# Five feed-forward stages by Strassen's seven products in a two-block transformer kernel

## Chip, cores and metric

One Trainium2 chip, one core. The metric is device microseconds of the whole program, median over runs.

## The reference, cut to what matters

Two transformer blocks follow one another on x of 512 tokens and 1024 features in fp32: a first block (sparse attention, a linear recurrence, a gated merge) with one feed-forward, then two layers of four-way mixed attention ("mix"), each between two feed-forwards. Five feed-forwards in all, each of the form

```
h = rms_norm(x, g)
x = x + half * (silu(h @ w_gate) * (h @ w_up)) @ w_down
```

with 1024 features and 2816 hidden ones; half is 1 in the first block and 0.5 later. After the feed-forward that ends a layer, x itself is normalized once more (`final_norm`).

## The kernel before, in words

Activations stand with features on the 128 partitions: xT is [128, 8, 512], eight feature tiles of 512 tokens. To keep fp32 accuracy, each operand of a matmul is split into a high part (rounded by a ScalarE copy to fp32r) and a low part (VectorE: the value less its high part), and a product is three matmuls: high by high, high by low, low by high (`feat`, L144 to 152).

`stream` (L116) loads weights in pieces of [128, 1024], 512 KB (L126, on SyncE's queue), casts 512 columns at a time to `hi` (L133, ScalarE) and subtracts to `lo` (L135, VectorE; GpSimd while a mix runs). Its tiles raw (2 buffers), hi and lo (4 each) are of the pool `wp`, opened once for the whole kernel, so the weights of a stage can be loaded and split while the stage before still computes.

`ffn` (L515) opens a pool `ph_f`. For each of 11 units of 256 hidden features it streams the gate's and the up's block and makes for each 2 x 8 x 3 = 48 matmuls of 512 columns; from PSUM, VectorE multiplies by the norm's factor rB (L531, L537), ScalarE takes Silu (L532), VectorE multiplies both (L538) and the result is split into fh and fl (L219, L220), 22 tiles each of ph_f. Then down: for each of four pairs of output tiles 22 x 2 x 3 = 132 matmuls in two PSUM banks, added to xT (L547 or L549). Behind each xT tile, the next stage's norm squares it, adds the square to acc on GpSimd (L233) and splits the scaled tile to xh and xl (L237, L238); at the end `norm_r` or, behind the second feed-forward of a layer, `final_norm` makes the row factors: a sum over partitions on TensorE (L203), a power on GpSimd (L196), a broadcast on TensorE (L212) and a copy (L215). `final_norm` then multiplies all eight xT tiles by rF, a tile of ph_f (L620).

The order on each engine is written down ahead of the run by a planner that follows program order, priorities (`high_priority`) and its own estimate of durations; on the chip each engine keeps to that order. Pools are placed as on a stack: `mix` opens ph_x, `ffn` opens ph_f, one after the other at the same depth. PSUM has eight banks; tags mm, s and t have two each.

Of the kernel before, what the change touches and what calls it, by code (L numbers as in the profile page):

```python
# [8 lines left out]
FT = mybir.dt.float32  # L9
# [9 lines left out]
T = 512  # L19
# [73 lines left out]
class Kern:  # L93
# [212 lines left out]
    def block1(self):  # L306
# [35 lines left out]
        with tc.tile_pool(name="ph_m", bufs=1, side="right") as pm:  # L342
            mh, ml = pm.tile([128, 8, T], FR, name="mh"), pm.tile([128, 8, T], FR, name="ml")
            skews = self.skews(pm)
            next(skews)
            with left_, tc.tile_pool(name="ph_t", bufs=1) as pt:
                self.merge(pt, got, ah, al, lh, ll, mh, ml)
            px = self.st.enter_context(tc.tile_pool(name="xT", bufs=1))
            self.xT = xT = px.tile([128, 8, T], FT, name="xT")
            nc.sync.dma_start(xT, I["xT"])  # L350
            whole(skews)
            self.outproj(I["w_o"], mh, ml, self.norm("norm2", 0))
        self.dump("x1", xT)
        self.ffn(0, None, self.norm("ffn1", 0))
        self.dump("x2", xT)
# [5 lines left out]
    def norm(self, gname, g0):  # L361

        xh, xl = self.new_x()
        acc = self.new_acc()
        xT = self.xT

        def tile_done(k):
            self.norm_k(xT[:, k], k, self.col(gname, g0 + k), xh, xl, acc)

        def finish():  # L370
            self.xh, self.xl = xh, xl
            self.r, self.rB = self.norm_r(acc)
        return tile_done, finish
# [141 lines left out]
    def ffn(self, f, half, norm):  # L515

        tc, nc, I = self.tc, self.nc, self.I
        V, S, G = nc.vector, nc.scalar, nc.gpsimd
        xh, xl, rB, xT = self.xh, self.xl, self.rB, self.xT
        ks = [(k, k) for k in range(8)]  # L520
        with tc.tile_pool(name="ph_f", bufs=1) as pf:
            self.pf = pf
            fh = [pf.tile([128, n, T], FR, name=f"fh{i}") for i, n in enumerate((8, 8, 6))]
            fl = [pf.tile([128, n, T], FR, name=f"fl{i}") for i, n in enumerate((8, 8, 6))]
            for j in range(11):
                wg = self.stream(I["w_g"][f, j], 8, 256)
                wu = self.stream(I["w_u"][f, j], 8, 256)
                z = [pf.tile([128, T], FT, tag="z", name="z", bufs=3) for m in range(2)]
                ps = self.feat2(wg, ks, lambda k: xh[:, k], lambda k: xl[:, k])
                for m in range(2):  # L530
                    V.tensor_mul(z[m], ps[m], rB)  # L531
                    S.activation(z[m], z[m], AF.Silu)  # L532
                ps = self.feat2(wu, ks, lambda k: xh[:, k], lambda k: xl[:, k])
                for m in range(2):
                    k = 2 * j + m
                    u = pf.tile([128, T], FT, tag="u", name="u", bufs=2)
                    V.tensor_mul(u, ps[m], rB)  # L537
                    V.tensor_mul(u, u, z[m])  # L538
                    self.split(fh[k // 8][:, k % 8], fl[k // 8][:, k % 8], u)
            for j in range(4):  # L540
                w = self.stream(I["w_d"][f, j], 22, 256)
                ps = self.feat2(w, [(k, k) for k in range(22)], lambda k: fh[k // 8][:, k % 8],
                                lambda k: fl[k // 8][:, k % 8])
                for m in range(2):
                    k = 2 * j + m
                    if half is None:
                        V.tensor_add(xT[:, k], ps[m], xT[:, k])  # L547
                    else:
                        V.scalar_tensor_tensor(xT[:, k], ps[m], half, xT[:, k], op0=OP.mult, op1=OP.add)  # L549
                    norm[0](k)  # L550
            norm[1]()


    def block2(self):
# [3 lines left out]
        for l in range(2):  # L558
            self.dump(f"xf1_{l}", xT)
            norm = self.norm("ffn2", 8 * l)  # L560
            self.wide = False
# [10 lines left out]
    def final_norm(self, l):  # L572
# [6 lines left out]
        if not last:  # L579
            xh, xl = self.new_x()  # L580
            acc2 = []
            gg = self.sm.tile([128, 8], FT, tag="gg", name="gg")
            V.tensor_mul(gg, self.col("final", 8 * l, 8), self.col("ffn1", 8 * l + 8, 8))

        def tile_done(k):
# [10 lines left out]
            if k == 0:  # L596
                acc2.append(self.pf.tile([128, T], FT, name="acc2"))
# [3 lines left out]
            g = gg[:, k:k + 1]  # L601
            S.activation(xh[:, k, :], xk, AF.Copy, scale=g)
            V.scalar_tensor_tensor(xl[:, k, :], xk, g, xh[:, k, :].bitcast(FT), op0=OP.mult, op1=OP.subtract)

        def finish():
            rf = self.rstd(self.tokred(acc, self.ones, 1), 1024, 4, "rt")
            if not last:
# [5 lines left out]
                self.r, self.rB = r, self.bcast(r)  # L613
                self.xh, self.xl = xh, xl
            rB = self.bcast(rf, self.pf, "rF")
            for k in range(8):
# [9 lines left out]
    def mix(self, px, l, norm):  # L626
# [12 lines left out]
        def hot():  # L639
            return tc.high_priority(offset=1000)  # L640

        rows = tl("rows2", [128, ROWS["_2"]])
        nc.sync.dma_start(rows, I["rows2"][l].partition_broadcast(128))
# [27 lines left out]
        def sqp():  # L671
            return tl("sqp", [128, T], FT, 2)

# [94 lines left out]
        def ptile():  # L768
            return tl("P", [128, T], FT, 8)

# [81 lines left out]
        def wout_b(Y, sum_b):  # L852
# [14 lines left out]
            for j in range(4):  # L867
# [3 lines left out]
                for m in range(2):  # L871
                    k = 2 * j + m
                    with hot():
                        t = sqp()
                        V.tensor_mul(t, banks[j][m], rb)
                        V.tensor_add(xT[:, k], t, xT[:, k])
                        norm[0](k)


        def diff():  # L880
# [29 lines left out]
            def head(h):  # L910
# [31 lines left out]
                def soft(qb):  # L942
# [4 lines left out]
                    for m in range(2):  # L947
# [3 lines left out]
                        PE.matmul(ps, qT[:96, qb * 128:qb * 128 + 128], kT[:96], start=True, stop=True)  # L951
                        p = tl("P1", [128, T], FT, 2) if m else ptile()
                        V.tensor_tensor_reduce(p, ps, t["toep"][:, 384 - qb * 128:896 - qb * 128], 1.0, 3e38,
# [82 lines left out]
        def na():  # L1036
# [6 lines left out]
            def evac(tb, ps, rt):  # L1043
                v = tl("sqp", [128, 4, 128], FR, 2, name="vst")
                vevac(v, v4(ps), rt)
# [17 lines left out]
            def head(h):  # L1063
# [21 lines left out]
                def soft(cb):  # L1085
# [4 lines left out]
                    mn, sm, rc = (t["st"][:, i, cb:cb + 1] for i in range(3))  # L1090
                    B = tl("P1", [128, 8, 32], FT, 2, name="nab")
                    G.tensor_tensor(B, namask[:, cb, None, :].to_broadcast([128, 8, 32]), t["E"][:, :, o:o + 32],
# [588 lines left out]
def host(inputs):  # L1681
# [94 lines left out]
    for i, n in enumerate(("w_g", "w_u", "w_d")):  # L1776
        A[n] = np.stack([blocks(f[i], 256) for f in ff])
    A["rows2"] = np.stack([np.concatenate([x["mla_q_norm_2"][l][64:], x["mla_k_norm_2"][l][64:], x["gqa_q_norm_2"][l],
# [54 lines left out]
```

## Time and profile before

| | |
|---|---|
| median of 3 runs | 3131.63 us (3128.5 to 3133.9) |
| the profiled execution | 3132.92 us |
| its span, first to last instruction | 3131.1 us |
| mean granted TensorE clock | 0.983 |
| share of the span busy: PE, DVE, ACT, POOL | 97%, 55%, 44%, 24% |

Matmuls are pipelined, so the records of one engine overlap; the pace of matmuls is the distance of their starts. Idle time of an engine is noted with what ended it.

### The profile page before, as it was taken

How to read it: one execution, taken by the hardware profiler on the slowest of the kernel's cores; microseconds unless marked ns; L12 is line 12 of the kernel's file. 1: busy time of each engine (PE TensorE's matmuls, PEld its weight loads, DVE VectorE, ACT ScalarE, POOL GpSimd, SP SyncE). 2: the span in 40 equal slices, each digit the busy share in tenths (PEclk: the TensorE clock that was granted, in tenths of full speed). 3: DMA queues.
4: the chain of work that ended last, by engine and by line, in shares of the span. 5: the costliest groups of instructions: out<-in, count | busy, mean ns of one | idle time of the engine just before them, and what ended most of it. 6: DMA issues, size and time to landing. Idle time of an engine off the chain costs nothing.

```text
span 3131.1 us, 41177 instructions
## 1 busy us (share of the span) xinstructions
PE 3030.5 (97%) x15289; PEld 2549.3 (81%) x15289; DVE 1721.3 (55%) x3167; ACT 1389.4 (44%) x2707; POOL 736.7 (24%) x699
## 2 busy tenths in 40 slices
PE   7999999999999999999888999999999998999998
PEld 6888877888888888889877888888888987778886
DVE  7576785454444454337786554355443488665433
ACT  4577774343333333236765333333332577543322
POOL 0466650010000000028853000010000877210000
PEclk9999999999999999999989999999999998999999
DMA  4311112342333323333211323323233321122232
GB/s 135 105 60 58 48 41 76 100 143 95 100 98 91 101 95 95 101 112 100 79 32 41 101 95 98 99 89 99 97 96 97 111 90 47 41 88 94 95 101 81
DMA packets 105265, 275.81 MB, mean 88 GB/s; under 512 B 27172, under 2 KB 36900, under 8 KB 104904
## 3 DMA queue, kind: packets, MB, share of 16 engines
q1 hardware_dynamic: 105064, 273.18, 28.1%
q8 instruction: 120, 1.97, 0.3%
q14 instruction: 81, 0.66, 0.1%
HBM read 268.93 MB, written 6.80 MB: 88 GB/s over the span
## 4 chain that ended last, share of the span: by engine, by line
PE 73%; issue 13%; DVE 7%; ACT 3%; POOL 3%; DMA 1%; SPq 0%; DVEq 0%; POOLq 0%; ACTq 0%
PE ps_mm L150 7%; PE ps_mm L152 7%; PE ps_mm L151 7%; PE ps_s L151 6%; PE ps_s L150 6%; PE ps_s L152 6%; PE ps_t L152 6%; PE ps_t L150 6%; PE ps_t L151 6%; PE ps_mm L180 2%; PE ps_mm L181 2%; PE ps_mm L182 2%; DVE PTl L220 1%; PE ps_t L792 1%; POOL lo L135 1%
## 5 line engine op out<-in xcount | busy, mean ns | idle before, releaser
L133 ACT ACTIVATE hi<-raw 128x512 fp32r<-128x512 f32 (+4 forms) x952 | 594.5, 627 | 1362.0 <-PE ps_mm L151 410.5
L135 DVE TENSOR_TENSOR lo<-raw,hi 128x512 fp32r<-128x512 f32 (+1 forms) x782 | 547.0, 701 | 934.1 <-ACT hi L133 925.5
L150 PE MATMUL ps_mm<-xh,hi 128*128 128x512 f32 x784 | 309.8, 395 | 1.4 <-ACT hi L133 1.2
L152 PE MATMUL ps_mm<-xh,lo 128*128 128x512 f32 x784 | 307.0, 394 | 3.1 <-POOL lo L135 3.1
L151 PE MATMUL ps_mm<-xl,hi 128*128 128x512 f32 x784 | 307.7, 392 | 0.0
L233 POOL TENSOR_TENSOR acc<-acc,sq 128x512 f32<-128x512 f32 x42 | 62.5, 1488 | 1037.8 <-issue 525.7
L152 PE MATMUL ps_s<-xh,lo 128*128 128x512 f32 (+1 forms) x664 | 259.7, 392 | 6.3 <-DVE lo L135 6.3
L150 PE MATMUL ps_s<-xh,hi 128*128 128x512 f32 (+1 forms) x664 | 256.9, 392 | 7.4 <-ACT hi L133 7.4
L151 PE MATMUL ps_s<-xl,hi 128*128 128x512 f32 (+1 forms) x664 | 260.6, 392 | 3.0 <-DVE xl L238 2.9
L181 PE MATMUL ps_mm<-lo,xh 128*128 128x256 f32 (+1 forms) x896 | 255.9, 288 | 2.0 <-DVE lo L135 2.0
L180 PE MATMUL ps_mm<-hi,xh 128*128 128x256 f32 (+1 forms) x896 | 255.4, 289 | 1.3 <-ACT tk L661 1.0
L182 PE MATMUL ps_mm<-hi,xl 128*128 128x256 f32 (+1 forms) x896 | 253.7, 286 | 0.1
L135 POOL TENSOR_TENSOR lo<-raw,hi 128x512 fp32r<-128x512 f32 (+2 forms) x170 | 225.5, 1334 | 114.6 <-ACT hi L133 107.9
L150 PE MATMUL ps_t<-xh,hi 128*128 128x512 f32 x608 | 236.9, 390 | 0.0
L151 PE MATMUL ps_t<-xl,hi 128*128 128x512 f32 x608 | 236.7, 389 | 0.0
L152 PE MATMUL ps_t<-xh,lo 128*128 128x512 f32 x608 | 235.9, 390 | 0.3 <-DVE lo L135 0.3
L152 PEld LDWEIGHTS ps_mm<-xh,lo 128*128 128x128 f32 x784 | 148.2, 189 | 35.1 <-POOL lo L135 4.1
L180 PEld LDWEIGHTS ps_mm<-hi,xh 128*128 128x128 f32 x896 | 171.9, 193 | 5.0 <-issue 1.7
L181 PEld LDWEIGHTS ps_mm<-lo,xh 128*128 128x128 f32 x896 | 172.5, 193 | 4.0 <-DVE lo L135 2.5
L150 PEld LDWEIGHTS ps_mm<-xh,hi 128*128 128x128 f32 x784 | 148.6, 190 | 32.9 <-ACT hi L133 1.9
L182 PEld LDWEIGHTS ps_mm<-hi,xl 128*128 128x128 f32 x896 | 171.9, 193 | 1.7 <-DVE xl L238 0.5
L151 PEld LDWEIGHTS ps_mm<-xl,hi 128*128 128x128 f32 x784 | 148.7, 190 | 30.1
(526 smaller groups left out, 6646.7 us busy)
## 6 DMA issues: line engine op xcount, KB each, us to landing
raw<-in_w_g SPq DMA_DIRECT2D x110, 512.0 KB
raw<-in_w_u SPq DMA_DIRECT2D x110, 512.0 KB
raw<-in_w_d SPq DMA_DIRECT2D x108, 512.0 KB
raw<-in_w_o SPq DMA_DIRECT2D x24, 512.0 KB
raw<-in_w_c SPq DMA_DIRECT2D x16, 512.0 KB
raw<-in_w_m SPq DMA_DIRECT2D x16, 512.0 KB
raw<-in_w_a SPq DMA_DIRECT2D x12, 512.0 KB
raw<-in_w_d SPq DMA_DIRECT2D x20, 256.0 KB
```

The lines of the kernel that those rows point to most:

```text
L133: nc.scalar.activation(hi[:, :c], x, AF.Copy)
L135: eng.tensor_tensor(lo[:, :c], x, hi[:, :c].bitcast(FT), op=OP.subtract)
L150: mm(ps, wh, mh(km), start=s, stop=False)
L151: mm(ps, wh, ml(km), start=False, stop=False)
L152: mm(ps, wl, mh(km), start=False, stop=e)
L180: mm(out[tb], h, wh, start=k == 0 and tb % 2 == 0, stop=False)
L181: mm(out[tb], h, wl, start=False, stop=False)
L182: mm(out[tb], o, wh, start=False, stop=k == K - 1 and tb % 2 == 1)
L220: self.nc.vector.tensor_sub(lo, src, hi.bitcast(FT))
L233: (eng or nc.gpsimd).tensor_tensor(acc, acc, sq, op=OP.add)
L792: PE.transpose(ps[:, qb * 128:qb * 128 + 128], P[qb][:, kb * 128:kb * 128 + 128], ident)
```

## The change

All five feed-forwards compute gate and up in Winograd's form of Strassen's scheme. Per unit, the weights are four blocks a11, a12, a21, a22 (row: which of the unit's two hidden tiles, gate beside up; column: even or odd feature tiles), each [128, 1024], 512 KB. The activations are four blocks too (even or odd feature tile, first or second half of the tokens), and of them seven combinations are made once per stage by `combine`, which takes the place of `norm_split` ahead of every feed-forward: per pair of feature tiles two scaled copies, four subtractions of 256 columns, and the splits. Seven products of 24 matmuls with 256 columns each take the place of 96 matmuls with 512 columns.

- Weight sums: s1 = a21 + a22 and s3 = a21 - a11 by accumulating DMAs issued by GpSimd, s2 = s1 - a11 and s4 = a12 - s2 on VectorE.
- Low parts: of products 3 (a12) and 6 (a22) by a ScalarE copy of the negated high part and an accumulating DMA; of the other five by VectorE.
- The products lie in banks mm and s; VectorE, ScalarE and GpSimd combine them to the tiles c, and `act` does the multiplication by rB, Silu, the product (GpSimd) and the split.
- The tiles raw2 (a11, a22), S (the sums), wh and wl (high and low parts, 3 buffers each), c and fh, fl (8 each instead of 22) are of ph_f. a12 and the down weights go through `wp`.
- Down runs in five passes over 4, 4, 4, 4 and 6 hidden tiles, put between the products of the units after, each adding to xT.
- In the first unit the first three products issue the first three quarters of the features ahead of the last quarter.
- `combine` has its tiles x and t in the pool of the stage before: ph_o, ph_x (tq, tk) or ph_f (c). `final_norm` has acc2 and rF in buffers of S and raw2.
- A pool x3, open from the first feed-forward on, holds the three additional blocks; in `mix` the buffers P, P1 and sqp move into it, with the same counts.

```diff
+    def combine(self, k, xk, g, xc):
+        V, S = self.nc.vector, self.nc.scalar
+        p = k // 2
...
+        S.activation(x[:, 2 * (k % 2):2 * (k % 2) + 2], xk.rearrange("p (a b) -> p a b", a=2), AF.Copy, scale=g)
+        if k % 2 == 0:
+            self.split(hi[0][:, p, 0], lo[0][:, p, 0], x[:, 0])
+            return
+        self.split(hi[0][:, p, 1:3], lo[0][:, p, 1:3], x[:, 2:4])
+        t = self.t4("t")
+        V.tensor_sub(t[:, 0], x[:, 1], x[:, 0])
+        V.tensor_sub(t[:, 1], x[:, 3], t[:, 0])
+        V.tensor_sub(t[:, 2], x[:, 3], x[:, 1])
+        V.tensor_sub(t[:, 3], x[:, 2], t[:, 1])
+        self.split(hi[0][:, p, 3], lo[0][:, p, 3], t[:, 0])
+        self.split(hi[1][:, p], lo[1][:, p], t[:, 1:4])
...
     def ffn(self, f, half, norm):
...
+            def load(u, i):
+                pool, tag, n = (pf, "raw2", 3) if i % 3 == 0 else (pf, "S", 4) if i == 2 else (self.wp, "raw", 2)
+                t = pool.tile([128, 2 * T], FT, tag=tag, name=f"A{i}", bufs=n)
+                with tc.high_priority(offset=6000):
+                    nc.sync.dma_start(t, I["w_gu"][f, u, i])
+                return t
+            def prod(x, c, ranges=((0, 4),), dma=False):
+                h, o = (pf.tile([128, 2 * T], FR, tag=n, name=n, bufs=3) for n in ("wh", "wl"))
+                with tc.high_priority(offset=3000):
+                    S.activation(h, x, AF.Copy)
+                    if dma:
+                        S.activation(o, x, AF.Copy, scale=-1.0)
+                        G.dma_start(o, x, accum_op=OP.add)
+                    else:
+                        V.tensor_sub(o, x, h.bitcast(FT))
+                nbank[0] += 1
+                ps = self.bank(("mm", "s")[nbank[0] % 2])
+                for a, b in ranges:
+                    for i in range(2):
+                        out = ps[:, i * 256:i * 256 + 256]
+                        for p in range(a, b):
+                            sl = slice((4 * i + p) * 128, (4 * i + p) * 128 + 128)
+                            mm(out, h[:, sl], xh[c](p), start=i == 0 and p == 0, stop=False)
+                            mm(out, h[:, sl], xl[c](p), start=False, stop=False)
+                            mm(out, o[:, sl], xh[c](p), start=False, stop=i == 1 and p == 3)
+                    yield
...
+            def unit(u):
+                a11, s1, a22 = load(u, 0), load(u, 2), load(u, 3)
+                s2, s3 = stile(), stile()
+                with early():
+                    G.dma_start(s1, a22, accum_op=OP.add)
+                    S.activation(s3, a11, AF.Copy, scale=-1.0)
+                    G.dma_start(s3, I["w_gu"][f, u, 2], accum_op=OP.add)
+                    V.tensor_sub(s2, s1, a11)
+                r = ((0, 3), (3, 4)) if u == 0 else ((0, 4),)
+                heads = [prod(x, c, r) for x, c in ((a11, 0), (s1, 3), (s2, 4))]
...
+            d = iter(())
+            for u in range(11):
+                if u % 2 == 0 and u:
+                    d = down(list(range(2 * u - 4, 2 * u + (0 if u < 10 else 2))), u == 10)
+                for i, _ in enumerate(unit(u)):
+                    if i in ((2, 6) if u < 10 else (2,)):
+                        next(d, None)
+            whole(d)
             norm[1]()
```

## Rows read from the trace of the kernel before

**Rows 1.** The page, part 1: busy time, share and instructions of each engine.

```profile
PE 3030.5 (97%) x15289; PEld 2549.3 (81%) x15289; DVE 1721.3 (55%) x3167; ACT 1389.4 (44%) x2707; POOL 736.7 (24%) x699
```

**Rows 2.** Windows: stretch, its length, busy time of each engine, granted clock, DMA share, GB/s.

```profile
800.00:1000.00 200.00, 200.00 (x884) 165.63 (x883) 87.31 (x128) 62.86 (x104) 4.28 (x3) 1.00 0.32 97
...
1020.00:1050.00 30.00, 30.00 (x142) 25.09 (x141) 12.77 (x18) 10.22 (x17) 4.02 (x3) 1.00 0.27 92
```

**Rows 3.** Timeline of PE, first feed-forward: start us, us, what; ten consecutive matmuls.

```profile
899.84 0.39 PE L150 MATMUL ps_mm<-xh,hi 128*128 128x512 f32 x1
...
901.88 0.39 PE L150 MATMUL ps_mm<-xh,hi 128*128 128x512 f32 x1
```

**Rows 4.** Timeline of PE, projections of the first mix: 27 consecutive matmuls.

```profile
1429.77 0.28 PE L180 MATMUL ps_mm<-hi,xh 128*128 128x256 f32 x1
...
1432.88 0.28 PE L182 MATMUL ps_mm<-hi,xl 128*128 128x256 f32 x1
```

**Rows 5.** Groups by line and form: xcount, busy us, mean ns of one, idle before.

```profile
L133 ACT ACTIVATE hi<-raw 128x512 fp32r<-128x512 f32 x934 | 586.9, 631 | 1350.4 <-PE ps_mm L151 410.5 <-PE ps_s L151 403.6 <-PE ps_t L151 401.5
L135 DVE TENSOR_TENSOR lo<-raw,hi 128x512 fp32r<-128x512 f32 x776 | 545.4, 705 | 932.8 <-ACT hi L133 924.3 <-PE ps_t L152 2.2
...
L220 DVE TENSOR_TENSOR PTl<-ps_t,PTh 128x256 fp32r<-128x256 f32 x32 | 13.4, 418 | 13.2 <-ACT PTh L219 12.7
```

**Rows 6.** Instructions of a line, 1024 columns: ns min/median/max, first and last start us.

```profile
L502 ACT ACTIVATE yT<-yT x4: 1059/1060/1061, 166.7 to 413.4; 128x1024 f32<-128x1024 f32 x4
...
L704 DVE TENSOR_TENSOR tk<-tk,rk x2: 1226/1226/1227, 1426.0 to 2470.3; 128x1024 f32<-128x1024 f32 x2
```

**Rows 7.** The same view of lines 238 and 233.

```profile
L238 DVE SCALAR_TENSOR_TENSOR xl<-xT,cols,xh x48: 734/1324/1780, 638.0 to 2765.3; 128x512 fp32r<-128x512 f32 x48
...
L233 POOL TENSOR_TENSOR acc<-acc,sq x42: 1284/1542/1673, 638.5 to 2764.8; 128x512 f32<-128x512 f32 x42
```

**Rows 8.** The page, part 3: DMA queue, packets, MB, share of 16 engines' span.

```profile
q1 hardware_dynamic: 105064, 273.18, 28.1%
```

**Rows 9.** The chain that ended last, 70 to 110 us: start us, us, transfer.

```profile
74.65 4.06 DMA raw<-in_w
...
81.23 3.94 DMA raw<-in_w_lx
```

**Rows 10.** Timelines of ACT and DVE, entry of the fourth feed-forward.

```profile
2094.68 0.59 ACT L215 COPY rB<-ps_n 128x512 f32<-128x512 f32 x1 [0.94 <-PE ps_n L212]
...
2097.42 0.69 DVE L135 TENSOR_TENSOR lo<-raw,hi 128x512 fp32r<-128x512 f32 x1 [2.96 <-ACT hi L133]
...
2101.21 5.39 DVE L620 SCALAR_TENSOR_TENSOR xT<-xT,cols,rF 128x512 f32<-128x512 f32 x8 [0.38 <-ACT rF L215]
...
2107.72 1.28 DVE L531 TENSOR_TENSOR z<-ps_mm,rB 128x512 f32<-128x512 f32 x2
```

**Rows 11.** Timelines of PE and SP, entry of the second mix.

```profile
2434.83 0.39 PE L152 MATMUL ps_s<-fh,lo 128*128 128x512 f32 x1
...
2435.25 0.33 SPq L643 DMA_DIRECT2D rows<-in_rows  x1
```

**Rows 12.** Timeline of PE, end of the second mix: the last output matmul.

```profile
2748.20 0.63 PE L152 MATMUL ps_mm<-yhl,lo 128*128 128x512 f32 x1
```

**Rows 13.** Windows of 5 us, entry of the fifth feed-forward; columns as in rows 2.

```profile
2745.00:2750.00 5.00, 5.00 (x14) 3.87 (x14) 5.00 (x6) 3.13 (x6) 3.28 (x2) 0.59 0.00 0
2750.00:2755.00 5.00, 4.25 (x17) 2.85 (x16) 5.00 (x8) 2.85 (x5) 1.85 (x2) 1.00 0.00 0
2755.00:2760.00 5.00, 4.11 (x17) 2.75 (x16) 5.00 (x6) 2.45 (x5) 2.78 (x2) 1.00 0.39 108
```

**Rows 14.** Timelines of PE, POOL and ACT, end of the third feed-forward.

```profile
2086.52 0.94 PE L203 MATMUL ps_n<-ones,acc 128*128 128x1 f32 x8
...
2088.01 1.46 POOL L196 TENSOR_TENSOR rt<-nm,mhalf 128x4 f32<-128x4 f32 x1 [4.72 <-DVE nm L194]
...
2099.50 1.05 PE L212 MATMUL ps_n<-ident,rt 128*128 128x128 f32 x8
2100.59 0.59 ACT L215 COPY rF<-ps_n 128x512 f32<-128x512 f32 x1 [0.49 <-PE ps_n L212]
```

More of the change, by code (lines that the diff above doesn't have):

```diff
@@ L517, in ffn @@
         tc, nc, I = self.tc, self.nc, self.I
[L518 to L520 removed]
+        V, S, G, mm = nc.vector, nc.scalar, nc.gpsimd, nc.tensor.matmul
+        rB, xT = self.rB, self.xT
         with tc.tile_pool(name="ph_f", bufs=1) as pf:
             self.pf = pf
[L523 to L547, printed above, removed]
[L548 to L550 removed]
@@ new lines, in unit @@
+            def unit(u):
[8 more added lines that the diff above has]
+                heads = [prod(x, c, r) for x, c in ((a11, 0), (s1, 3), (s2, 4))]
+                c1, c2 = (pf.tile([128, 2, 2, 256], FT, tag="c", name="c", bufs=3) for _ in range(2))
+                if u == 0:
+                    for g in heads:
+                        next(g)
+                ps = whole(heads[0])
+                with soon():
+                    S.copy(c1[:, 0], ps)
+                yield
+                ps = whole(heads[1])
+                with soon():
+                    S.copy(c2[:, 1], ps)
+                yield
+                ps = whole(heads[2])
+                with soon():
+                    V.tensor_add(c1[:, 1], ps, c1[:, 0])
+                yield
+                a12 = load(u, 1)
+                ps = whole(prod(a12, 1, dma=True))
+                with soon():
+                    V.tensor_add(c1[:, 0], ps, c1[:, 0])
+                yield
+                ps = whole(prod(s3, 5))
+                with soon():
+                    V.tensor_sub(c2[:, 0], c1[:, 1], ps)
+                    G.tensor_tensor(c1[:, 1], c1[:, 1], c2[:, 1], op=OP.add)
+                    G.tensor_tensor(c2[:, 1], c2[:, 1], c2[:, 0], op=OP.add)
+                yield
+                s4 = stile()
+                with early():
+                    V.tensor_sub(s4, a12, s2)
+                ps = whole(prod(s4, 2))
+                with soon():
+                    V.tensor_add(c1[:, 1], ps, c1[:, 1])
+                    act(u, 0, c1)
+                yield
+                ps = whole(prod(a22, 6, dma=True))
+                with soon():
+                    V.tensor_add(c2[:, 0], ps, c2[:, 0])
+                    act(u, 1, c2)
+                yield
@@ new lines, in down, with run @@
+            def down(part, last):
+                n = len(part)
+                w, banks = {}, {}
+                def run(j, a, b, tag="t"):
+                    if j not in w:
+                        w[j] = self.stream(I["w_d"][f, j][:, part[0] * 256:(part[-1] + 1) * 256], n, 256)
+                        banks[j] = [self.bank(tag) for _ in range(2)]
+                    for i in range(a, b):
+                        for m in range(2):
+                            self.feat(banks[j][m], lambda k: pick(w[j](k), m), [(i, part[i])], lambda k: fh[k],
+                                      lambda k: fl[k], start=i == 0, stop=i == n - 1)
+                    if b < n:
+                        return
+                    for m in range(2):
+                        k = 2 * j + m
+                        V.scalar_tensor_tensor(xT[:, k], banks[j][m], 1.0 if half is None else half, xT[:, k],
+                                               op0=OP.mult, op1=OP.add)
+                        if last:
+                            norm[0](k)
+                if not last:
+                    for j in range(4):
+                        run(j, 0, n)
+                        yield
+                    return
+                run(0, 0, 4)
+                yield
+                run(1, 0, 4, "mm")
+                run(2, 0, 4, "s")
+                for j in range(3):
+                    run(j, 4, n)
+                run(3, 0, n)
```

82 lines of the change are left out of this document (63 added, 19 removed).

## Prediction

> **What bounds the kernel now.** I read the page's busy line first. TensorE (PE) is busy 97% of the span, VectorE (DVE) 55%, ScalarE (ACT) 44%, GpSimd (POOL) 24% [rows 1]. Then a window inside the first feed-forward (FFN): PE has no gap in 200 us at a granted clock of 1.00, DVE is busy 44% and ACT 31% of it; the window over the step from the first FFN to the second has no gap either [rows 2]. So in the five FFNs only the number and the pace of the matmuls count, and a weight transfer or a cast costs nothing while it stays ahead. The pace is read from start to start in the PE timeline, not from the 0.39 or 0.28 us of a record, which overlap. With 512 columns it is (901.88 - 899.84) / 9 = 226.7 ns [rows 3]; with 256 columns, in the projections of a mix stage, (1432.88 - 1429.77) / 26 = 119.6 ns [rows 4]. Two halves cost 239.2 ns, 5.5% more than a whole one.
>
> **What is removed.** Gate and up are 11 units of 96 matmuls of 512 columns, 1056 x 226.7 = 239.4 us of an FFN. They become 11 units of seven products of 24 matmuls with 256 columns, 1848 x 119.6 = 221.0 us. Seven eighths of the columns would be 12.5% less, the shorter matmuls leave 7.7%: 18.4 us of an FFN, **92 us of five**. Down keeps its 528 matmuls; in five passes instead of one they take as long. The Trainium skill, TensorE: Matmul & The Clock Gate, Back-to-back issue gap, has columns / 2.4 GHz plus 2.5 ns for a matmul: 215.8 and 109.2 ns. By that rule the gain would be 26 us of an FFN, 130 of five, and the sum below 38 us lower; the two rows are some 11 ns above it at both sizes, and I go by the rows.
>
> **What a unit adds on the other engines.** A unit with its share of down is 168 x 119.6 + 48 x 226.7 ns = 31.0 us of PE. A 1024-wide cast is 1.06 us on ACT, a 1024-wide subtraction 1.23 us on DVE [rows 6]; 512-wide ones 0.63 and 0.70 [rows 5].
> - ACT: 7 high parts, 2 negated copies, 1 negated block, at 1.06; 2 copies from PSUM, 2 Silu, 2 casts of the result and 4 of down at 0.63: 16.9 us, 55%.
> - DVE: 5 low parts, 2 weight sums and 2 scalings at 1.23; 5 combinations, 2 low parts, 4 of down, 3.6 additions to xT at 0.70: 21.3 us, 69%. Additions to xT are 40 instead of 8 an FFN.
> - POOL: 4 operations of 512 columns at 1.54 [rows 7] and 4 DMA issues. While POOL works on two tensors, DVE instructions on two tensors stretch: 0.73 us alone, median 1.32, 1.78 at worst [rows 7]. With 6.2 us of that, DVE comes to some 25 us, 82%.
> - DMA: 3.0 MB loaded and 2.0 MB accumulated. The queue moved 273 MB in 28.1% of the span, 310 GB/s while at work [rows 8]; 31 us hold 9.6 MB, enough even if an accumulated byte counts double.
>
> On average all stay under PE, so the steady state is hidden but for one wait. The low parts of products 3 (a12) and 6 (a22) come by accumulating DMA: two ACT copies, 2.1 us, then the transfer, and PE needs it at its third matmul. There are three buffers of high and low parts. Ahead of product 6 stand two products, 48 x 119.6 ns = 5.7 us, from the time its buffer is free; ahead of product 3 also a down pass of 5.4 us, from the third unit on. No DMA of POOL is in the trace. The nearest row is a 512 KB load on SP, 3.94 to 4.06 us from release to landing [rows 9]; as the accumulation reads two streams I bound it by that and by twice that. The stall of a unit then lies between 2.1 + 4.0 - 5.7 = 0.4 us and 4.4 us, or nothing where the down pass is put ahead. I take the row it is nearest to, 0.4 us: **+22 us** of 55 units; the ends are 0 and 240.
>
> **What stands on the path: the entry of an FFN.** Before, the weight tiles lie in a pool open for the whole kernel, so the next FFN's weights are on chip before the last down matmul. After, raw2, S, wh and wl lie in ph_f, opened anew for each FFN on the bytes of the stage before. Two places show what such a pool waits for. Mix opens ph_x on those bytes: its first DMA leaves at 2435.25, with the last fh matmul (2434.83), though fh0, the tile at the pool's bottom, holds the first 8 of 22 slices and was read for the last time 14 x 6 = 84 matmuls, 19 us, earlier [rows 11]. And z, a tile of the fourth FFN's ph_f, is first written at 2107.72, directly behind the eight multiplications by rF, a tile of the old ph_f, though its input rB stood at 2095.3 and DVE idled 2.96 us in between [rows 10]. So each tile of the new pool waits for every user of the old one. For the first, second, third and fifth FFN the last user is the new combine step, which reads its x and t tiles in that pool; for the fourth it is the multiplication by rF.
>
> From that release R: a11 lands after 4.0 us, the second half MB and a22 1.65 us behind each other by the queue's rate: 7.3; the summing DMA onto s1, bounded as above, 4.0: 11.3; its cast 1.06 and low part 1.23: product 1 runs in earnest at 13.6 and product 2 ends at 13.6 + 2 x 2.87 = 19.3. Three products are 8.6 us of work, so R + 10.7 us is the start that an undisturbed FFN would have had. Product 0 falls into the wait, even at 1.2 GHz, the level that part of the window behind such a wait was granted (0.59 on average) [rows 13].
>
> R itself, by combine's DVE work: a pair of feature tiles takes low parts of 256, 512, 256 and 768 columns and four subtractions of 256, at 0.42 [rows 5], 0.70, 0.42, 0.96 (between the neighbours) and 4 x 0.42: 4.2 us, with the two additions to xT 5.6.
> - First FFN: only the last pair is late, R = 6 us past the last matmul. Loss **17 us**.
> - Second: the last pass ends three pairs 2.7 us apart, so DVE runs behind, R = 9. Loss **20**.
> - Fourth: R lies behind combine, two rounds of sum (0.94), pow (1.46), broadcast (1.05) and copy (0.59) and 5.4 of multiplications, 9 + 1 + 14 = 24 [rows 10, 14]. Loss **35**.
> - Third and fifth, behind mix: DVE is already full there, 5.00 of 5 us [rows 13]; its last xl begins at 2765.3 [rows 7] and ends 1.3 us later. Eight of these go (8.6 us), four combines come (16.8): R = 2774.8, as if begun at 2785.5. Before, the last output matmul starts at 2748.2 [rows 12], and two windows of 5 us then hold 17 matmuls instead of 22 [rows 13], so it is as if begun at 2751. Loss **34 each**.
>
> Together **+140 us**; the floor, with the summing DMA hidden, is 5 x 5.6 = 28 less. What is renamed in mix (P, sqp, P1 as slots of x3 with the same counts) costs nothing: the same rotation hides it; without that cover a wait of the kind that mix has now, 0.5 to 3 us a time.
>
> **Sum.** On the profiled execution, 3132.9 us: 3132.9 - 92 + 22 + 140 = 3203; the median of the runs is 1.3 lower: **3202 us**.
>
> **Rivals.**
> - *Entries are hidden* (faster). The weights are prefetched after all, or the scheduler finds other room for ph_f: 3131.6 - 92 + 22 + 16 (the extra DVE work behind mix) = **3078 us**. For it: SP and the DMA queues are free at every entry, the products' first three quarters of features are issued apart from the last as if weights were there early. Against it: the two waits of [rows 10, 11]. Chance 0.25.
> - *Accumulating DMAs come late all along* (slower still): at 2.4 us a unit, the middle of my bounds, 110 us more, **3312 us**. It decides from 3.6 us of transfer on, as every us beyond counts 55 times. For it: POOL's queue is in order, so a DMA behind an addition that waits for DVE waits too. Chance 0.18. The Trainium skill, DMA: Bandwidth & Descriptors, SWDGE vs HWDGE vs iDMA, says that POOL writes such descriptors into SBUF and that DVE can lock it out of there meanwhile; that would feed this rival, and no row here shows such a DMA.
> - *A draw*: every release comes as early as the first FFN's, 5 x 17 = 85 us, and the units stall by 0 to 22 us: 3132.9 - 92 + 85 = 3126 to 3148, with 3131.6 among them. It needs DVE to finish combine behind mix 17 us sooner than its load there says. Chance 0.07.
> - That the change does not do what it says, I give no weight: the count of matmuls follows from the loops.
>
> **Chances.** Forecast 0.50, the others 0.25, 0.18, 0.07. Faster is the first rival, slower the forecast and the second. The forecast's own range is 3150 to 3265; to leave no more than 2 in 10 out, the range reaches down into the hidden entries and up to the late DMAs: 3065 to 3310. A measurement of this kernel can tell about 0.2%, 6 us, from no change.
>
> **What would show it.** Right: PE windows of the first 30 us of each FFN with 10 to 35 us idle, the first in_w_gu load of an FFN issued after the last combine instruction or the last multiplication by rF, then 168 matmuls a unit at 119 to 120 ns. Wrong: loads of the next FFN issued while the down matmuls of the old one run; PE waits of more than 1 us a unit on wl inside an FFN (the second rival); or a pace of the products other than 119.6 ns.

## The result and the profile after

The changed kernel takes **3333.91 us** (median of 4 runs, 3331.87 to 3336.24), 1.0653 times the kernel before (95% interval 1.0634 to 1.0671; 3130.07 us beside it): 204 us more, where 70 more were forecast, and above the range's upper end of 3310. The direction was right, the size was not. The profiled execution has a span of 3330.1 us against 3131.1.

The page's busy times and DMA queues after, against [rows 1, 8]:

```profile
PE 3020.4 (91%) x19249; PEld 2721.9 (82%) x19249; DVE 2216.2 (67%) x3447; ACT 1764.0 (53%) x3007; POOL 1291.1 (39%) x1139
...
q1 hardware_dynamic: 105064, 273.18, 26.5%
q0 software_dynamic: 31680, 115.36, 19.0%
```

PE is busy 10 us less than before and idle 209 us more. The second queue is new: the 220 accumulating DMAs of GpSimd. Windows show where PE is idle (stretch, length, busy time of each engine, clock, DMA share, GB/s): the first entry, a stretch inside the first FFN, the entries of the third and fourth FFN:

```profile
666.00:715.00 49.00, 34.04 (x220) 31.59 (x219) 26.55 (x30) 22.78 (x29) 13.82 (x12) 0.79 0.66 171
...
880.00:1000.00 120.00, 118.95 (x817) 110.78 (x816) 85.17 (x93) 57.99 (x74) 35.94 (x28) 1.00 0.66 158
...
1773.00:1844.00 71.00, 33.18 (x186) 30.80 (x185) 42.86 (x60) 30.54 (x47) 25.66 (x16) 0.64 0.46 112
2178.00:2250.00 72.00, 34.18 (x208) 31.81 (x207) 41.66 (x59) 29.15 (x42) 17.63 (x15) 0.67 0.41 101
```

and 90 us of the first units of the first and third FFN, behind their first products:

```profile
700.00:790.00 90.00, 79.40 (x553) 74.53 (x552) 62.23 (x63) 45.54 (x57) 28.62 (x24) 0.94 0.72 169
...
1820.00:1910.00 90.00, 81.85 (x586) 78.75 (x585) 59.52 (x61) 47.40 (x60) 30.59 (x27) 0.92 0.74 177
```

Inside an FFN PE misses 1 us in 120. At the entries of the third and fourth FFN it misses more than half of some 70 us, and over the first units still a tenth, at a granted clock of 0.94 and 0.92. With the start of the last matmul of a stage as its end, the stages last, in us:

| stage | before | after | difference |
|---|---|---|---|
| up to the last mh matmul of `outproj` | 668.6 | 666.8 | -1.8 |
| first, second FFN | 360.9, 360.9 | 384.3, 391.2 | +23.4, +30.3 |
| first mix | 318.0 | 330.8 | +12.8 |
| third, fourth FFN | 363.6, 362.9 | 405.4, 409.4 | +41.8, +46.5 |
| second mix | 313.4 | 321.6 | +8.2 |
| fifth FFN | 364.3 | 401.0 | +36.8 |
| behind it | 18.7 | 19.6 | +0.9 |

PE's waits by what released them, in sum, times and the longest (us):

```profile
PE ps_n L203 <- POOL acc L233: 56.9, 4, 22.2
PE ps_mm L601 <- ACT wh L588: 28.6, 9, 5.5
PE ps_s L601 <- ACT wh L588: 26.9, 8, 11.1
PE ps_n L203 <- DVE acc L752: 19.6, 2, 17.3
PE ps_mm L603 <- DMA wl<-A: 18.4, 13, 5.1
PE ps_s L603 <- DMA wl<-A: 18.3, 14, 3.8
```

Two families: the norm's sum (L203), which stands in PE's order ahead of the products, and the products' high and low parts. A wait names its last releaser only; behind `wh L588` stands another DMA. (Line numbers are those of the kernel that ran. In the changed one L575 loads a block of weights, L588 casts a high part, L593 subtracts a low part on VectorE, L590 and L591 make one by copy and DMA, L625 sums s1, L626 and L627 make s3, L601 to L603 are the products.) The timeline of the first entry tells (start, length, engine and line; behind the bracket the idle time before it; the last outproj matmul starts at 666.82):

```profile
673.16 0.94 DVE L220 TENSOR_TENSOR x3l<-t,x3h 128x768 fp32r<-128x768 f32 x1
...
674.26 16.98 SPq L575 DMA_DIRECT2D A<-in_w_gu  x6
...
678.18 1.06 ACT L588 ACTIVATE wh<-A 128x1024 fp32r<-128x1024 f32 x1 [5.35 <-DMA A<-in_w_gu]
...
680.51 1.07 POOL L627 DMA_DIRECT2D S<-in_w_gu  x1 [5.25 <-ACT S L626]
...
681.30 1.20 POOL L625 DMA_DIRECT2D A<-A  x1
...
688.52 1.06 ACT L588 ACTIVATE wh<-A 128x1024 fp32r<-128x1024 f32 x1 [7.86 <-DMA A<-A]
...
689.63 0.58 PE L601 MATMUL ps_mm<-xh,wh 128*128 128x256 f32 x1 [4.75 <-ACT wh L588]
...
693.19 0.86 POOL L591 DMA_DIRECT2D wl<-A  x1 [10.69 <-ACT wl L590]
```

The release is nearly where the prediction put it: combine's last instruction ends at 674.1 and the first load leaves at 674.26, R = 7.3 against 6. a11 is there 3.9 us later. Then s1's summing DMA, written behind that of s3 on GpSimd, leaves at 681.30, 7.2 us behind the release, where the forecast had it (7.3). It lands just before 688.52, 14.4 us behind the release instead of 11.3: the transfer took 7.2 us and not 4.0. The median of its kind is 4.6; s3's was under way beside it, and how much of the rest is due to that was not tried. By issues (count, size, median us to landing):

```profile
wl<-A POOLq DMA_DIRECT2D x110, 512.0 KB, 5.4
...
S<-in_w_gu POOLq DMA_DIRECT2D x55, 512.0 KB, 7.4
A<-A POOLq DMA_DIRECT2D x55, 512.0 KB, 4.6
```

### The profile page after: what moved, and what is told of

The parts are those of the page before. It is cut to its first block, busy times and chain, and to the rows that moved or that the text cites. A ratio compares the mean times of both kernels' runs of the same rounds, so it can differ in the third digit from the quotient of the medians.

```text
span 3330.1 us, 50223 instructions
## 1 busy us (share of the span) xinstructions
PE 3020.4 (91%) x19249; PEld 2721.9 (82%) x19249; DVE 2216.2 (67%) x3447; ACT 1764.0 (53%) x3007; POOL 1291.1 (39%) x1139
## 5 line engine op out<-in xcount | busy, mean ns | idle before, releaser
L133 ACT ACTIVATE hi<-raw 128x512 fp32r<-128x512 f32 (+3 forms) x512 | 314.5, 620 | 470.1 <-PE ps_t L151 187.3
L135 DVE TENSOR_TENSOR lo<-raw,hi 128x512 fp32r<-128x512 f32 (+1 forms) x342 | 295.5, 868 | 156.4 <-ACT hi L133 152.4
L588 ACT ACTIVATE wh<-A 128x1024 fp32r<-128x1024 f32 x220 | 231.5, 1055 | 311.2 <-PE ps_mm L602 146.7
L591 POOL DMA_DIRECT2D wl<-A x110 | 97.7, 888 | 693.9 <-ACT wl L590 664.2
L151 PE MATMUL ps_t<-fl,hi 128*128 128x512 f32 x760 | 297.3, 391 | 0.0
L152 PE MATMUL ps_t<-fh,lo 128*128 128x512 f32 x760 | 295.7, 389 | 0.0
L150 PE MATMUL ps_t<-fh,hi 128*128 128x512 f32 x760 | 295.5, 393 | 0.0
L601 PE MATMUL ps_mm<-xh,wh 128*128 128x256 f32 x920 | 268.8, 292 | 28.6 <-ACT wh L588 28.6
L603 PE MATMUL ps_mm<-xh,wl 128*128 128x256 f32 x920 | 270.6, 294 | 26.1 <-DMA wl<-A 16.3
L601 PE MATMUL ps_s<-xh,wh 128*128 128x256 f32 x840 | 244.6, 291 | 25.5 <-ACT wh L588 25.5
L602 PE MATMUL ps_mm<-xl,wh 128*128 128x256 f32 x920 | 267.4, 291 | 0.0
L603 PE MATMUL ps_s<-xh,wl 128*128 128x256 f32 x840 | 246.4, 293 | 17.8 <-DMA wl<-A 12.3
L593 DVE TENSOR_TENSOR wl<-S,wh 128x1024 fp32r<-128x1024 f32 x165 | 208.8, 1266 | 55.9 <-ACT wh L588 55.4
L588 ACT ACTIVATE wh<-S 128x1024 fp32r<-128x1024 f32 x165 | 174.2, 1056 | 73.3 <-PE ps_mm L602 40.8
L603 PE MATMUL ps_s<-x3h,wl 128*128 128x256 f32 x720 | 207.1, 288 | 6.4 <-DMA wl<-A 6.1
L601 PEld LDWEIGHTS ps_mm<-xh,wh 128*128 128x128 f32 x920 | 184.1, 200 | 32.7 <-ACT wh L588 30.5
```

The costliest lines, as they stand in the source:

```text
L133: nc.scalar.activation(hi[:, :c], x, AF.Copy)
L135: eng.tensor_tensor(lo[:, :c], x, hi[:, :c].bitcast(FT), op=OP.subtract)
L150: mm(ps, wh, mh(km), start=s, stop=False)
L151: mm(ps, wh, ml(km), start=False, stop=False)
L152: mm(ps, wl, mh(km), start=False, stop=e)
L588: S.activation(h, x, AF.Copy)
```

## Experiments

Two theories stood at the start. *Pool*: the entries are long because ph_f waits for every user of the pool below it. *Queues*: they are long because of the order on GpSimd, ScalarE and PE and because of the accumulating DMAs. In each FFN I read the starts of the units (their first product) and add up the five FFNs. "Pace" is 20.1 us for a unit without a down pass, 31.0 with one; the last column runs from unit 10's first product to the last matmul. Matmuls of neighbouring products are interleaved, so the edges of units are good to about 1 us in a sum.

| sum of five FFNs, us | to the first product | unit 0 | unit 1 | unit 2 | units 3 to 9 | rest |
|---|---|---|---|---|---|---|
| at the pace | 0 | 100.5 | 100.5 | 155 | 1085 | 263 |
| changed kernel | 138.0 | 175.0 | 139.6 | 169.7 | 1105.6 | 263.5 |
| e1 waits by tile | 132.5 | 176.0 | 139.6 | 169.2 | 1104.3 | 263.5 |
| e2 first sums on DVE | 138.6 | 131.8 | 145.8 | 167.9 | 1103.5 | 263.2 |
| e3 low parts on DVE | 137.6 | 155.3 | 132.5 | 146.9 | 1087.8 | 263.1 |
| e4 acc on DVE | 121.2 | 176.3 | 138.3 | 163.7 | 1101.4 | 263.5 |
| e5 shared pool | 109.6 | 171.8 | 137.1 | 170.3 | 1105.0 | 263.5 |
| e6 no such DMA | 137.9 | 116.8 | 127.1 | 146.6 | 1087.8 | 263.1 |
| e7 e2 to e5 together | 92.4 | 130.2 | 127.3 | 145.4 | 1087.8 | 263.1 |
| e8 none in units 0 to 2 | 137.9 | 116.8 | 123.9 | 146.1 | 1108.0 | 263.2 |

**e1: the waits of the pool taken away.**

```diff
-        with tc.tile_pool(name="ph_f", bufs=1) as pf:
+        with tc.tile_pool(name="ph_f", bufs=1, reuse_waits="tile") as pf:
```

> Edit: the pool ph_f waits byte by byte (each tile only for the earlier users of its own bytes) instead of for every user of the pool below it; the order of instructions on every engine is the same as in the changed kernel. Pool theory (the entries are long because the first weight loads wait for the last combine instruction or the last multiplication by rF): loads of the second to fifth FFN leave before that, the way from the release to product 1 in earnest, 15.5 us, shrinks by at least the 4 us of the first load and up to the whole 15 us: 16 to 60 us less, 3274 to 3318 us, likeliest 3290. Queue rival (the products stand behind the norm's sum in TensorE's queue, and the summing DMAs behind the additions to acc in GpSimd's, so early weights find no one to use them): under 12 us less, 3322 to 3334 us.

Measured: 3323.63 us (3322.22 to 3328.45), 10 less. The pool theory misses, the queue rival holds. In the second FFN the four loads that the release had held leave 23 us earlier than in the changed kernel, counted from the last matmul before, and nothing follows from it. The timelines around that entry, first of e1 (last matmul 1048.23), SP, ScalarE and PE:

```profile
1038.01 4.37 SPq L575 DMA_DIRECT2D A<-in_w_gu  x6
...
1066.26 0.59 ACT L215 COPY rB<-ps_n 128x512 f32<-128x512 f32 x1 [4.05 <-PE ps_n L212]
1066.74 1.06 ACT L588 ACTIVATE wh<-A 128x1024 fp32r<-128x1024 f32 x1
...
1067.85 0.58 PE L601 MATMUL ps_s<-xh,wh 128*128 128x256 f32 x1 [1.63 <-ACT wh L588]
```

then of the changed kernel (last matmul 1051.17):

```profile
1060.35 1.87 PE L203 MATMUL ps_n<-ones,acc 128*128 128x1 f32 x8 [8.79 <-POOL acc L233]
1067.08 2.07 PE L212 MATMUL ps_n<-ident,rt 128*128 128x128 f32 x8 [4.86 <-POOL rt L196]
1070.99 0.58 PE L601 MATMUL ps_s<-xh,wh 128*128 128x256 f32 x1 [1.83 <-ACT wh L588]
...
1066.26 1.75 SPq L575 DMA_DIRECT2D A<-in_w_gu  x4
```

The first product comes 19.6 and 19.8 us behind the last matmul. With the weights on chip, their cast still stands behind the norm's copy (L215) in ScalarE's order, and the products behind L203 and L212 in PE's.

**e5: one pool for two FFNs in a row**, so that the planner knows of no boundary and writes another order.

```diff
-        with tc.tile_pool(name="ph_f", bufs=1) as pf:
-            self.pf = pf
+        with ExitStack() as st:
+            if f in (0, 2, 4):
+                self.pf = self.pst.enter_context(tc.tile_pool(name="ph_f", bufs=1))
+            pf = self.pf
```

> Edit: one pool ph_f for the first and second FFN, and one for the third and fourth, instead of a new one each; nothing else. After the run with byte-wise waits (3323.6 us; in the second FFN all five weight blocks landed before the last matmul, and product 0 still came at 19.6 us instead of 19.8, since ScalarE's, GpSimd's and TensorE's written orders were as before) the theory is that the pool costs through the order that the planner writes: behind a new pool it puts casts, summing DMAs and products after the norm's chain. With the pool shared it can put them ahead: the second FFN's first product within 8 us of the last down matmul, the fourth's ahead of the 15.8 us of sum, power, broadcast and rF multiplications; 25 to 60 us less, 3274 to 3309 us. Rival (combine on VectorE, which ends 15 and 19 us behind the last matmul, sets the entry anyway): the second FFN gains under 5, the fourth up to 16: 3313 to 3330 us.

Measured: 3305.50 us (3300.72 to 3309.08), 28 less; the second FFN 368.2 instead of 391.2, the fourth 401.7 instead of 409.4. PE's timeline in the second FFN's entry:

```profile
1051.25 0.39 PE L152 MATMUL ps_t<-fh,lo 128*128 128x512 f32 x1
1051.48 0.28 PE L603 MATMUL ps_s<-xh,wh 128*128 128x256 f32 x1
```

0.23 us lie between the last down matmul and the first product. So the pool did cost some 20 us here, and the order that was written with it in mind has a part in that: e1 took the wait away and kept the order, and gained nothing here; e5 takes both away. Whether the new order with the old wait would gain anything was not tried. In the fourth FFN the norm's chain still stood ahead of the products (first product at 30.9 instead of 39.5).

**e2 and e3: the accumulating DMAs taken away in part.**

```diff
+                    if u == 0:
+                        V.tensor_sub(s3, s1, a11)
+                        V.tensor_add(s1, s1, a22)
+                    else:
...
```

is e2, and e3, for a22 likewise:

```diff
-                ps = whole(prod(a12, 1, dma=True))
+                ps = whole(prod(a12, 1, dma=False))
```

> Edit: in the first unit of each FFN, s3 = a21 - a11 and s1 = a21 + a22 are made by VectorE instead of one ScalarE copy and two accumulating DMAs; all other units unchanged. Summing-DMA theory: at the entry s1's DMA is issued 7.2 us after the release and has landed 14.4 us after it, while a21 and a22 are there at about 8; two VectorE instructions of 1.23 us give s1 at about 10.5: 4 us less in each FFN, and the rest of the unit earlier by as much: 12 to 25 us less in all, 3309 to 3322 us. Rival (the second and third unit, late behind the same GpSimd queue, lose what the first gains): under 6 us less.

Measured: 3298.94 us (3293.51 to 3303.26), 35 less, more than expected: unit 0 shrinks by 43 us in five FFNs, unit 1 gives 6 back. In e2's first entry (last matmul 666.79, release 674.2) the same sum on VectorE still waits for a22 to land:

```profile
681.59 1.22 DVE L627 TENSOR_TENSOR A<-A,A 128x1024 f32<-128x1024 f32 x1 [0.20 <-DMA A<-in_w_gu]
```

The changed kernel's DMA, which left at 681.30, thus lost next to nothing in GpSimd's queue; what e2 saves at this entry is chiefly its landing.

> Edit: the low parts of products 3 and 6 by VectorE like the other five, in all units, instead of a ScalarE copy and an accumulating DMA; the sums of weights still by DMA. Theory that the low parts' DMAs cost little in the steady state (0.3 us a unit in units 3 to 9) but hold up the first three units of each FFN (6.2 us from the ScalarE copy's end to the landing, in GpSimd's queue): 10 to 50 us less, 3284 to 3324 us. Rival (VectorE, 67% busy over the span and fuller inside a unit, becomes the bound with 2.5 us more in 31): 0 to 60 us more.

Measured: 3267.01 us (3265.01 to 3271.17), 67 less, also more than expected: 20 in unit 0, 30 in units 1 and 2, 18 in units 3 to 9. VectorE does not become the bound; its window stands with that of e6 below.

**e6: no accumulating DMA at all, e8: none in units 0 to 2.** e6 is the edits of e2 and e3 for every unit, e8 both for u < 3.

> Edit: no accumulating DMA at all: the low parts of products 3 and 6, and the sums s1 and s3, by VectorE in every unit. Alone, the low parts on VectorE gave 3267.0 us and the first unit's sums on VectorE 3298.9 (66.9 and 35.0 less). If both are separate costs of the DMAs, and VectorE has room for 5 us more in a unit of 31.1 us: 3232 us, 3222 to 3242. If VectorE fills (it then has about 26 us of work in 31 without stretch): units 3 to 9 go from 31.08 to over 32 us, 40 us or more come back: over 3265 us.

Measured: 3219.71 us (3216.02 to 3220.68), 114 less than the changed kernel. The same window inside the first FFN in e3, then in e6 (columns as above):

```profile
880.00:1000.00 120.00, 120.00 (x831) 112.33 (x830) 95.14 (x98) 53.57 (x70) 30.87 (x22) 1.00 0.43 114
```

```profile
880.00:1000.00 120.00, 120.00 (x836) 112.61 (x835) 96.82 (x102) 48.94 (x64) 23.71 (x16) 1.00 0.27 82
```

PE has no gap with DVE at 81%. And the first entry of e6, ScalarE's timeline:

```profile
681.33 1.06 ACT L588 ACTIVATE wh<-A 128x1024 fp32r<-128x1024 f32 x1 [4.91 <-DMA A<-in_w_gu]
682.29 0.57 ACT L215 COPY rB<-ps_n 128x512 f32<-128x512 f32 x1
686.14 1.06 ACT L588 ACTIVATE wh<-A 128x1024 fp32r<-128x1024 f32 x1 [3.28 <-DVE A L627]
```

Product 1's cast comes 4.8 us behind product 0's, with the DMAs 10.3 (678.18 and 688.52 above).

> Edit: in the first three units of each FFN no accumulating DMA (low parts and sums by VectorE); in the other eight all of them as in the changed kernel. Filling theory (the DMAs cost where the pipeline of three buffers is not yet full: the run without any of them is 58 us shorter in the first units, 36 in the second and third, 16 in the fourth to tenth): nearly all of the 114 us that the run without them gained, about 96: 3236 us, 3225 to 3247. Rival (the DMAs are late all along and only the place of the wait moves to the first units that use them): the fourth to sixth unit of each FFN lose what the first three gain, 3260 us or more.

Measured: 3245.01 us (3243.70 to 3250.19), 89 less, 78% of e6's gain. Units 3 to 9 take 1108 us, 2 more than in the changed kernel: the DMAs cost 20 us in those 35 units (1087.8 without them), and next to nothing that the first units gained is lost behind them. So the filling theory holds as to the place. Nor do the low parts' DMAs land later at the start. By issues of the changed kernel, units 0 to 2 of its first FFN (679 to 778 us), then units 3 to 9 (778 to 998):

```profile
wl<-A POOLq DMA_DIRECT2D x6, 512.0 KB, 5.7
...
wl<-A POOLq DMA_DIRECT2D x14, 512.0 KB, 6.6
```

What differs is how long PE waits for them. That it waits at the start because the buffers hold no lead yet is the reading that fits both; a run with more buffers was not made.

**e4: the additions to acc on VectorE.**

```diff
-            self.norm_sq(xT[:, k], k, acc)
+            self.norm_sq(xT[:, k], k, acc, self.nc.vector)
...
-                G.tensor_tensor(acc2[0], acc2[0], sq, op=OP.add)
+                V.tensor_tensor(acc2[0], acc2[0], sq, op=OP.add)
```

> Edit: the additions of the squares to acc (and acc2) ahead of an FFN on VectorE instead of GpSimd. Queue theory (the norm's sum on TensorE waits up to 22 us for GpSimd's additions, and VectorE's work stretches up to threefold beside them): the last combine and the sum come earlier, 15 to 40 us less, 3294 to 3319 us. Pool theory alone (VectorE's own combine work sets the release; seven more additions of 0.69 us lengthen it): from 10 us less, as the stretch goes, to 20 us more.

Measured: 3318.71 us (3310.38 to 3322.59), 15 less, at the edge of the queue theory; two of the four runs lie above its range. The stages say more: 17 us go ahead of the first products, 6 of them in the third FFN. What is removed there stands in the changed kernel's timeline behind the first mix, GpSimd, then PE (last matmul 1773.13):

```profile
1786.87 8.81 POOL L233 TENSOR_TENSOR acc<-acc,sq 128x512 f32<-128x512 f32 x2 [3.38 <-ACT sq L231]
...
1795.73 1.44 PE L203 MATMUL ps_n<-ones,acc 128*128 128x1 f32 x6 [22.21 <-POOL acc L233]
```

and VectorE beside it:

```profile
1792.54 0.67 DVE L220 TENSOR_TENSOR xl<-x,xh 128x512 fp32r<-128x512 f32 x1
1797.63 0.16 DVE L194 TENSOR_SCALAR nm<-ps_n 128x4 f32<-128x4 f32 x1 [4.42 <-PE ps_n L203]
1797.71 0.41 DVE L397 TENSOR_TENSOR t<-x,t 128x256 f32<-128x256 f32 x1
```

The small step L194 stands in VectorE's order ahead of the last combine instructions. It waits for PE, PE for GpSimd, so the release waits for an addition to acc.

**e7, e9, e10: what remains when the gains are put together.** e7 is e2, e3, e4 and e5; e9 has no accumulating DMA at all besides; e10 also writes the norm's last step behind the products' heads:

```diff
+            if f in (0, 2):
+                self.pre()
+                self.late = norm[1]
+            else:
+                norm[1]()
```

> Edit: four edits together: low parts on VectorE, the first unit's sums on VectorE, additions to acc on VectorE, and the pool ph_f shared by two FFNs in a row. If their gains are separate: 3333.9 less 66.9, 35.0, 15.2 and what sharing gives (25 to 60): 3157 to 3192 us. If they remove the same waits more than once: 3195 to 3240 us. In neither case faster than the kernel before, as the entries of the first, third and fifth FFN keep some 20, 35 and 35 us.

Measured: 3188.77 us (3181.61 to 3193.90). The single gains (66.9, 35.0, 15.2, 28.4) give 3188.4. The total so looks like separate costs, but its parts do not: in the profiled executions the five FFNs gain 68, 41, 27 and 34 us one by one, 170 in sum, and 145 together. So some 25 us of the gains overlap, and that the total agrees to a microsecond is luck, with runs that spread over 12.

> Edit: all five FFNs without accumulating DMAs, additions to acc on VectorE, pool ph_f shared by two FFNs in a row. If the single gains add (114.2, 15.2 and 28.4): 3333.9 - 157.8 = 3176 us, 3168 to 3185; above the kernel before in any case by the long entries of the third, fourth and fifth FFN. If the sums' DMAs behind the first unit cost nothing once their low parts are gone: as the run with four edits, 3189.

Measured: 3186.71 us (3181.58 to 3191.33), nearer to the rival, with runs on both sides of 3185. Against e7 the medians differ by 2 us, less than the runs do, and units 3 to 9 take 1087.8 us in both: the sums' DMAs behind unit 0 cost no time that can be seen once the low parts are off GpSimd and the rest is mended.

> Edit: on top of the run with five FFNs without accumulating DMAs (3186.7 us): ahead of the second and fourth FFN the norm's last step (sum, power, broadcast; in the fourth also rF and its eight multiplications) is written behind the first three products' heads, so that TensorE's order has the products first. With the shared pool the second FFN's first product came 0.2 us behind the last matmul, the fourth's still at 26.3 us, behind sums that TensorE waited for up to 18 us. Order theory: the fourth FFN's first product comes with the first combinations, within 5 us, and 8 to 20 us of its entry go: 3166 to 3179 us. Rival (the products' last quarter of features, which combine finishes 18 us behind the last matmul, holds them as long): under 6 us less, 3181 to 3188.

Measured: 3181.53 us (3176.35 to 3185.86), 5 less, as the rival says, and not clear of the spread: beside the kernel before the ratio is 1.0159 (1.0135 to 1.0182) here and 1.0180 (1.0164 to 1.0196) in e9. The fourth FFN's first product now comes 0.2 us behind the last matmul instead of 26.3, yet the FFN takes 376.1 us instead of 379.2. The later products wait for VectorE, which has combine's work and the weights' low parts to do; PE's longest wait from 2080 to 2130 us:

```profile
PE ps_mm L608 <- DVE wl L598: 4.8, 1, 4.8
```

All five by Strassen stay 1.6% above the kernel before.

**h1: only the first two FFNs by Strassen**, in the kernel before, with the mended entries.

```diff
+            self.ffn_s(0, None, self.norm_c("ffn1", 0))
+            self.ffn_s(1, 0.5, self.norm("mix", 0))
```

> Edit: the kernel before, with only the first and second FFN by Strassen's products (no accumulating DMAs, additions to acc on VectorE, one pool for the two); third to fifth FFN, final_norm and both mixes as before. In the run with four edits the first FFN took 359.6 us and the second 354.7 (1.4 and 6.2 less than before), while mix and the later FFNs gave that back and more. If the pace's gain of 18.4 us a FFN outweighs an entry without mix or final_norm ahead of it: 6 to 16 us faster than before, 3115 to 3125 us, likeliest 3121. Rival (the mix behind such an FFN starts 4 to 5 us later whatever stands ahead of it, and the first FFN's entry is no cheaper): 3126 to 3135, no difference.

Measured: 3141.35 us (3137.06 to 3142.66), ratio 1.0032 (1.0020 to 1.0045): still 0.3% slower, past the rival's upper end. The two FFNs take 359.5 and 355.4 us, 7 less than before, but the first mix takes 329.0 instead of 318.0, though its code is that of the kernel before. The first 40 us of it, before and then in h1:

```profile
1390.00:1430.00 40.00, 39.79 (x328) 39.04 (x327) 13.45 (x24) 21.01 (x39) 34.00 (x22) 1.00 0.39 114
```

```profile
1385.00:1425.00 40.00, 37.92 (x311) 37.29 (x310) 16.36 (x24) 18.84 (x35) 35.74 (x23) 1.00 0.40 127
```

2 us are lost at its start, where the FFN's last pass ends three pairs of tiles close together; the other 9 are spread over a stage whose order the planner wrote anew. Why that order is worse was not tried. No version was found that beats the kernel before.

## Why the prediction was right, and where it failed

- **Pace, -92 us: right.** Units 3 to 9 of e3 and e6 take 1087.8 us, 31.08 a unit, against 31.0 worked out. The Trainium skill, TensorE: Matmul & The Clock Gate, Back-to-back issue gap, would have them 8% shorter (28.7 us, an estimate from its formula, which it gives for a matmul by itself); no run here has such units.
- **R, 92 us in sum: 21 short.** The first load leaves 7, 15, 28, 35 and 28 us behind the last matmul, 113 in sum, instead of 6, 9, 27, 24 and 27. In the fourth FFN combine ended 19 us behind it instead of 9, with VectorE instructions stretched beside GpSimd's. e4, without that, brings the first products 17 us earlier in sum. The loads of the third, fourth and fifth, whose stages before end at 1773.13, 2178.52 and 2909.48:

```profile
1801.61 1.75 SPq L575 DMA_DIRECT2D A<-in_w_gu  x4
...
2213.15 1.75 SPq L575 DMA_DIRECT2D A<-in_w_gu  x4
...
2937.45 1.75 SPq L575 DMA_DIRECT2D A<-in_w_gu  x4
```

- **From R to the end of product 2, 19.3 us each: 5 short, 24 in sum.** The step "the summing DMA onto s1, bounded as above, 4.0: 11.3" was mis-sized: the DMA left when it was to leave, 7.2 us behind the release, and took 7.2 us, near the upper of the two bounds (twice the load), where the lower had been taken. The other half is the clock: product 1, behind that wait, ran for the most part at 1.2 GHz.
- **"Three products are 8.6 us of work, so R + 10.7 us is the start that an undisturbed FFN would have had": this is the step that failed.** The FFN was not undisturbed behind product 2. From there to unit 9 the changed kernel loses 96 us, where 22 were given: 149 in units 0 to 9 above the pace and 138 to the first products, less 191 up to the end of product 2 (113 of R and 5 x 15.6). The other 75, beside the 21 that units 3 to 9 lose, lie in units 0 to 2: there PE waits for landings that it does not wait for later, and runs part of the time at the lower clock (0.94 and 0.92 in the windows above). Without the DMAs of these units (e8) 14 of the 75 are left; that the three buffers of high and low parts hold no lead yet is argued. I worked out the steady state's lead and took it for the start's, so the filling stood in the sum at nothing.
- **The 22 us of the steady state: near by luck.** With the measured landing of 5.4 us into the low parts its own formula gives 2.1 + 5.4 - 5.7 = 1.8 us a unit, 99 us in 55. Units 3 to 9 lose 0.6 a unit, so the lead must have been longer than the 5.7 us of the prediction, and two wrong sizes nearly cancel.
- **What waits at the entry.** The prediction gave the waits of the pool, and e1 shows that taking these alone away gains 10 us in all. The boundary between two FFNs, wait and written order together, costs 28 (e5), and the DMAs cost 114 (e6).
- **Mix: 21 us more, none of it predicted** beyond R. "The same rotation hides it" was said of the renamed tiles; h1, with mix as before, has 11 of its own behind a Strassen FFN, so the renaming need not be the reason; the cause stays open.
- **Rivals.** Late DMAs all along (3312) was nearest in size and wrong in place: e8 keeps them in 40 units and loses 20 us by them. Hidden entries (3078) was wrong, and e10 shows for the fourth FFN that weights and first product ahead of the norm are not enough: VectorE, with combine and the low parts, holds the products behind. A draw (3126 to 3148) lay 186 us too low.

In sum, against the forecast of +70: R 21, the way to product 2 24, filling 74 and mix 21 make 140; some 11 come off, as the five FFNs of the kernel before took 1812.6 us, 17 more than their own pace, of which the forecast had counted 6: 199 in the spans.

## What to carry to other kernels

A change that pays by the pace of a steady loop is paid for at every start of that loop: with five starts and 18 us to win at each, cost the filling of the buffers, product by product, before the steady state. Taking a wait away shows nothing while the order on the engines was written for it; change what the planner sees, and look whether the first dependent instruction moves. The accumulating DMAs here were nearly free only where other work covered their whole landing; on an engine with room (VectorE, 67%) the same sum took 1.2 us.

## What was not expected of the hardware

- **GpSimd's accumulating DMAs.** 512 KB, SBUF to SBUF, land a median 4.6 us after the issue with fp32 output and 5.4 into the low parts' tiles, from HBM 7.4; each issue above keeps GpSimd 0.9 to 1.2 us. A load on SP took 3.9 to 4.1 [rows 9].
- **GpSimd held off by VectorE.** Of the two additions to acc from 1786.87 on (8.81 us together, above; the median of all 42 is 1.4) the first took 7.5 us: VectorE ran instructions with two SBUF inputs without a gap until 1793.2, and the addition ended 1.1 us later. The other way round 256-column subtractions of 0.41 us took 1.48 beside GpSimd. The Trainium skill, SBUF — State Buffer, Who interferes with whom, says that a VectorE instruction with two SBUF inputs contends with a GpSimd one that reads SBUF; the trace agrees, and shows that a train of them can keep GpSimd waiting for 6 us.
- **The clock behind a wait.** The window 672 to 683, with 4.2 us of idle PE ahead of it and 2.1 and 1.9 inside, and that from 689 to 693, behind 4.75, were granted 0.50, 1.2 GHz; from 696 on it was 1.00 again:

```profile
672.00:683.00 11.00, 6.58 (x27) 5.91 (x28) 3.40 (x6) 3.31 (x4) 3.00 (x3) 0.50 0.56 197
689.00:693.00 4.00, 2.86 (x11) 2.57 (x12) 4.00 (x4) 3.89 (x5) 0.00 (x0) 0.50 0.50 145
696.00:700.00 4.00, 4.00 (x35) 3.88 (x34) 1.23 (x1) 1.94 (x3) 1.72 (x2) 1.00 1.06 188
```

Product 1 took 5.1 to 6.1 us at the five entries instead of 2.9: 2.2 to 3.2 us on the path each time, in the first entry with 0.5 of waiting for its low part in it.
